# Norms of two streams staggered, and adaLN vectors moved to VectorE, in a hybrid backbone kernel

## The chip, the core and the metric

The kernel runs on one core of a Trainium2 chip. The metric is the device time of one execution, in microseconds, the median of several runs. Engine names in the profile: PE is the matrix engine (TensorE), PEld its weight load, DVE is VectorE, ACT is ScalarE, POOL is GpSimd, SP issues the DMAs.

## The reference

Two layers work on 512 tokens of width 1024: 256 latent tokens (stream 0) and 256 context tokens (stream 1). Every sub-layer modulates its input with adaLN vectors that come from a conditioning vector, one for each stream, and ends in a layer norm:

```python
def macaron_ffn(h, shift, scale, gate, w_in, w_out, g, b):
    y = swiglu(modulate(h, shift, scale), w_in, w_out)       # silu(a) * b, hidden width 2816
    return layer_norm(DN_ALPHA * h + 0.5 * gate * y, g, b)
# layer: FFN -> mixers (HGRN2 | Hyena | windowed attention, merged by gates, one output projection) -> FFN
```

All sums are in float32. The output is the latent stream after two layers, so the second layer's mixer output and second FFN have only 256 columns.

## The kernel before, in words

Activations lie transposed: eight tiles of 128 channels by 512 tokens (`ah`), the streams side by side in the columns. A float32 product is made of three matmuls of a faster format, with weights and activations split in a high and a low part: `hi` is a rounded copy by ACT (L130), `lo` the rest by DVE (L132), and `mm3` (or L530, L531, L533 in `projO`) multiplies hi by hi, hi by lo and lo by hi. Split weights lie in three buffers of 1024 columns each for `hi` and `lo`.

An FFN runs twice over half of the hidden width. In each half 11 hidden blocks are made: two projections of 24 matmuls (a `pj` bank each), silu on ACT (L476), the product with the second bank on DVE (L477), and the split of the result (`g`). Then come eight output blocks d of 33 matmuls (L141 to L143), whose residual is added by DVE (L366). In the second half the residual also collects the sums for the norm.

`norm` then takes the token means of the sum and the squares with matmuls one column wide (L389), the mean for all columns (L423), rstd on ACT, DVE and POOL (L426), and its broadcast (L461). DVE subtracts and scales (L411, L438), ACT modulates and makes the rounded `uh` (L350, L352), DVE the rest `ul` (L357), POOL the rescaled residual (L449). While this chain runs, PE works on adaLN groups, the only work that doesn't need the normalized tokens.

One adaLN group is 512 of a layer's 9216 modulation values, for both streams. It can be made in two ways. `ada_group` lets PE multiply 8 weight slabs of 128 × 512 (L293), and PE transposes the result (L321). `ada_pairs` lets DVE multiply and add slab by slab into one accumulator for each stream (L266), two groups at a time, and PE only adds up the partitions of four accumulators with a vector of ones (L273) and transposes (L279). The second form is a generator that `pull` moves on by a step or two after each hidden block and output block. Of 36 groups, 14 go this way, 18 go by PE in the norms and at fixed places of FFNs (the `fill` table), and 4 of the first layer are made at the start.

The program is written as a list of operations, and a scheduler sets the order on each engine from its own costs; HOIST gives priority to the chains of the mixers. Inside `manual_schedule` the written order holds: in the kernel before, for PE in `norm` alone. The Hyena filters of both layers (`filters`) are made during layer 0's first FFN.

Of the kernel before, what the change touches and what calls it, by code (L numbers as in the profile page):

```python
# [16 lines left out]
P = 128  # L17
# [10 lines left out]
PAIR0 = ((6, 7), (8, 9), (13, 14))  # L28
HOLES = (3, 0, 0, 2)
BG = (2, 1)  # L30
LAG = 4
SKIP = (1, 2, 3)
# [45 lines left out]
class Net:  # L78
    def __init__(self, ctx, tc, a, out):
        self.tc, self.nc, self.a, self.out = tc, tc.nc, a, out  # L80
        self.uid = 0
        self.now, self.chains = 0.0, []
        ep = lambda **k: ctx.enter_context(tc.tile_pool(**k))
# [50 lines left out]

    def split(self, src, hi, lo):
        self.nc.scalar.activation(hi, src, AF.Copy)
        self.nc.vector.tensor_tensor(lo, src, hi, ALU.subtract)
# [32 lines left out]

    def pull(self, n):
        self.slot += 1
        if self.slot not in self.bg_skip:
            for _ in range(n):
                next(self.bg, None)
# [74 lines left out]
    def ada_pairs(self, l, gs, mods):  # L250
# [3 lines left out]
        for pair in gs:  # L254
            acc = []
            for g in pair:
                acc += [self.slab("W", name="acc") for _ in range(2)]
                for k in range(KD):
                    w = self.slab("EH"[k % 2], name="adaw")
                    nc.sync.dma_start(out=w, in_=self.a["ada_w"][l, g, k])  # L260
                    for t, s in zip(acc[-2:], range(2)):
# [5 lines left out]
                    if k % 2:  # L267
# [7 lines left out]
            sb = self.slab("T", name="ada")  # L275
            nc.scalar.activation(sb, p, AF.Copy)
            tr = self.pbank("ph")
            for b in range(4):
                nc.tensor.transpose(tr[:, b * P:(b + 1) * P], sb[:, b * P:(b + 1) * P], self.ident)  # L279
            v = tr.rearrange("p (b g s x) -> p g b s x", b=4, g=2, s=2)  # L280
            for i, g in enumerate(pair):
                bias = self.par("ada_b", l * 72 + g * 4, 4)
                nc.vector.tensor_tensor(mods[:, g * 4:g * 4 + 4, :], v[:, i, :, :, 0],
                                        bias.unsqueeze(2).to_broadcast([P, 4, 2]), ALU.add)
# [106 lines left out]
    def norm(self, l, i, ah, TT, st, mods_next, ish, keep=True, out=None, fill=()):  # L391
        nc = self.nc
        nb = TT // P
        units, end = [], None
        for f in fill:
            x = self.ada_group(*f)
            units += [(x, 1), end, (x, 1), (x, 1), (x, 1)] if end else [(x, 1)] * 4
            end = (x, 0)
        units += [end] if end else []

        def more(n):
            while units and n >= units[0][1]:
                x, m = units.pop(0)
                next(x, None)
                n -= m
# [8 lines left out]
        with self.tc.manual_schedule(engines={mybir.EngineType.PE}), self.tc.issue_after(self.last_mm.ins):  # L414
            more(HOLES[0])
            for tb in range(nb):
                self.token_mean(st["stat"][:, tb:tb + 1], st["s1"], tb, False, False)
            more(HOLES[1])
            for tb in range(nb):
                self.token_mean(st["stat"][:, 4 + tb:5 + tb], st["sq"], tb, False, tb == nb - 1)  # L420
            more(HOLES[2])
# [7 lines left out]
            more(HOLES[3])  # L429
# [25 lines left out]
        return u + [self.low(x, TT) for x in pend]  # L455
# [10 lines left out]
    def ffn(self, l, i, u, ah, TT, gate, extra=None, pre=None):  # L466
# [3 lines left out]
        hg_done = False  # L470
        for half in range(2):
            g = []

            def finish(pa, pb):
                s = self.slab("T", name="silu")
                nc.scalar.activation(s[:, :TT], pa[:, :TT], AF.Silu)  # L476
                nc.vector.tensor_tensor(s[:, :TT], s[:, :TT], pb[:, :TT], ALU.mult)  # L477
# [5 lines left out]
            while j < HALF:  # L483
# [5 lines left out]
                if n == 3:  # L489
                    banks = self.projO(pre, u, [TT] * 6)  # L490
                elif n == 2:
                    banks = self.projO([w(q) for q in range(3)], u, [TT] * 3)
                    finish(*banks[:2])
                    banks = banks[2:] + self.projO([w(3)], u, [TT], "ph")
# [5 lines left out]
                self.pull(BG[0])  # L500
# [7 lines left out]
            for d in range(KD):  # L508
                if half and d == KD - 1:
                    self.squares(st, TT)  # L510
# [8 lines left out]
                self.pull(BG[1])  # L519
# [45 lines left out]
    def hgrn_proj(self, l, h, u, NQ, outer):  # L565
        nc = self.nc
        i = 4 + 4 * h
        if outer:
            ws = [self.wload(self.a["mix_w"][l, i + q], tags=(None, "QQ", "FF")[q],
                             marks=self.marks if q in PIN else None) for q in range(3)]  # L570
            pz = self.projO(ws, u, (T, T, NQ))
        else:
            pz = [self.projT(l, i + r, u, T) for r in range(2)]
        f, k = self.wide("F", name="f"), self.wide("F", name="k")
        for r in range(2):
            col = l * 8 + r * 4 + h
            c = slice(r * T, (r + 1) * T)
            nc.scalar.activation(f[:, c], pz[r], AF.Sigmoid)
            nc.scalar.activation(k[:, c], pz[r], AF.Sigmoid, scale=-1.0)
# [3 lines left out]
        pq = pz[2] if outer else self.projT(l, i + 2, u, NQ)  # L583
        q = self.slab("S", name="q")
        nc.scalar.activation(q[:, :NQ], pq[:, :NQ], AF.Copy)
        pg = self.projT(l, i + 3, u, NQ, "ph" if outer else "pj")
# [477 lines left out]
    def mixer(self, l, u, ah, TT, gate):  # L1064
# [31 lines left out]
        def proj(h):  # L1096
            hp.append(self.hgrn_proj(l, h, u, TT, h == 0))
# [34 lines left out]
        for d in range(KD):  # L1132
            if d == KD - 1:
                self.squares(st, TT)
# [4 lines left out]
    def run(self):  # L1139
# [21 lines left out]
        for d in range(KD):  # L1161
# [7 lines left out]
            if d < 2:  # L1169
# [3 lines left out]
            (0, 0): [lz(ada, 0, 4), lz(ada, 0, 5), None, self.tables_a] + [None] * F0 + [lz(self.filters, 0)] + [None] * F1 +  # L1173
                    [self.tables_b, lz(ada, 0, 15), lz(self.filters, 1)],
            (1, 0): [None] + [lz(ada, 1, 15)],
        }
        bg = {(0, 0): self.ada_pairs(0, PAIR0, mods[0]),
              (0, 1): self.ada_pairs(1, [(1, 2), (3, 7)], mods[1]),
              (1, 0): self.ada_pairs(1, [(8, 9), (13, 14)], mods[1])}
        for l in range(DEPTH):  # L1180
            TT = T if l < DEPTH - 1 else L
            self.bg, self.slot, self.bg_skip = bg.get((l, 0), iter(())), 0, SKIP
            st = self.ffn(l, 0, u, ah, T, lambda: self.mod_cols(mods[l], 2), fill.get((l, 0)), pre if l == 0 else None)
            u = self.norm(l, 0, ah, T, st, mods[l], 3, fill=[(l, g, mods[l]) for g in (10, 11, 12)])
            st = self.mixer(l, u, ah, TT, self.mod_cols(mods[l], 5))
            u = self.norm(l, 1, ah, TT, st, mods[l], 6,
                          fill=[(l, 16, mods[l]), (l, 17, mods[l])] + ([(l + 1, 0, mods[l + 1])] if l < DEPTH - 1 else []))
            self.bg, self.slot, self.bg_skip = bg.get((l, 1), iter(())), 0, SKIP
            st = self.ffn(l, 1, u, ah, TT, lambda: self.mod_cols(mods[l], 8), fill.get((l, 1)))
            if l < DEPTH - 1:  # L1190
# [130 lines left out]
```

## Time and profile before

| | |
|---|---|
| median of 3 runs | 2385.11 us (2383.44 to 2387.33) |
| profiled execution | 2383.82 us, span 2382.0 us |
| granted PE clock, mean | 0.994 of full |
| PE, DVE, ACT, POOL busy | 98%, 60%, 41%, 7% of the span |
| PE waits for ACT's copy of adaLN sums (L321) | 9.7 us in 13 waits |
| PE waits for rstd (L461) | 3.9 us in 3 waits |
| DMA | 360.41 MB, mean 151 GB/s |

Busy time of a pipelined engine counts overlapping instructions once; the busy time of one matmul row is longer than its distance to the next, and the distance is what a matmul costs. A wait is idle time ahead of an instruction, with what ended it.

### The profile page before, as it was taken

The numbers are of one execution on the slowest core, as the hardware profiler recorded it, in microseconds if no ns is written. First come the engines' busy times: TensorE is split into PE (matmuls) and PEld (weight loads), VectorE is DVE, ScalarE is ACT, GpSimd is POOL, SyncE is SP. The second block draws the span as 40 slices with busy tenths as digits, with TensorE's granted clock in tenths as the row PEclk, the third lists the DMA queues.
The fourth block names the chain that finished last, engine by engine and source line by source line (L and its number), as shares of the span: only waits on it lengthen the run. The fifth ranks groups of instructions, "written<-read, shape, count | busy, mean of one in ns | idle before, by whom it ended". The sixth has DMA issues, their size and how long they took to land.

```text
span 2382.0 us, 34116 instructions
## 1 busy us (share of the span) xinstructions
PE 2343.4 (98%) x13112; PEld 1971.4 (83%) x13112; DVE 1440.5 (60%) x2403; ACT 970.3 (41%) x1663; POOL 170.3 (7%) x158
## 2 busy tenths in 40 slices
PE   8999999999999999999999999999999999999998
PEld 4778778699888888867888877878887999998998
DVE  3647848656877665776433357363346687776555
ACT  3424324444654433343222234222225466645443
POOL 1003002210010000010000001000002111000000
PEclk9999999999999999999999999999999999999999
DMA  9435734723223445765332247243224344694564
GB/s 365 139 102 172 233 97 121 263 67 105 77 80 128 154 137 190 254 207 156 108 121 93 83 139 251 90 149 106 92 86 137 118 129 138 197 320 153 171 198 125
DMA packets 153314, 360.41 MB, mean 151 GB/s; under 512 B 16576, under 2 KB 38208, under 8 KB 153152
## 3 DMA queue, kind: packets, MB, share of 16 engines
q1 hardware_dynamic: 153152, 358.24, 46.2%
q8 instruction: 103, 1.69, 0.3%
q14 instruction: 59, 0.48, 0.1%
HBM read 331.96 MB, written 26.21 MB: 150 GB/s over the span
## 4 chain that ended last, share of the span: by engine, by line
PE 94%; DMA 2%; DVE 2%; ACT 1%; issue 1%; SPq 1%; POOL 0%; ACTq 0%; DVEq 0%
PE pj L530 18%; PE pj L531 18%; PE pj L533 18%; PE pj L141 7%; PE pj L143 7%; PE pj L142 7%; PE ph L632 2%; PE pj L551 1%; PE pj L552 1%; PE pj L553 1%; PE ph L293 1%; PE pa L1006 1%; PE pa L873 1%; PE ph L678 1%; PE pa L997 1%
## 5 line engine op out<-in xcount | busy, mean ns | idle before, releaser
L132 DVE TENSOR_TENSOR lo<-raw,hi 128x1024 fp32r<-128x1024 f32 (+1 forms) x455 | 524.6, 1154 | 451.1 <-ACT hi L130 450.2
L530 PE MATMUL pj<-uh,hi 128*128 128x512 f32 (+1 forms) x2096 | 752.5, 359 | 4.6 <-ACT uh L352 3.0
L533 PE MATMUL pj<-ul,hi 128*128 128x512 f32 (+1 forms) x2096 | 749.2, 358 | 1.1 <-DVE ul L357 1.1
L531 PE MATMUL pj<-uh,lo 128*128 128x512 f32 (+1 forms) x2096 | 749.5, 358 | 0.0
L130 ACT ACTIVATE hi<-raw 128x1024 fp32r<-128x1024 f32 (+1 forms) x455 | 446.4, 982 | 602.3 <-issue 251.2
L530 PEld LDWEIGHTS pj<-uh,hi 128*128 128x128 f32 x2096 | 396.6, 189 | 74.5 <-issue 8.6
L533 PEld LDWEIGHTS pj<-ul,hi 128*128 128x128 f32 x2096 | 396.1, 189 | 59.3 <-DVE ul L357 2.5
L531 PEld LDWEIGHTS pj<-uh,lo 128*128 128x128 f32 x2096 | 396.4, 189 | 56.8 <-issue 2.1
L142 PE MATMUL pj<-g,hi 128*128 128x512 f32 (+1 forms) x704 | 255.7, 363 | 0.0
L143 PE MATMUL pj<-g,lo 128*128 128x512 f32 (+1 forms) x704 | 255.5, 363 | 0.0
L141 PE MATMUL pj<-g,hi 128*128 128x512 f32 (+1 forms) x704 | 255.4, 364 | 0.0
L141 PEld LDWEIGHTS pj<-g,hi 128*128 128x128 f32 x704 | 132.8, 189 | 23.7 <-issue 1.7
L143 PEld LDWEIGHTS pj<-g,lo 128*128 128x128 f32 x704 | 132.9, 189 | 22.3 <-DVE ah L366 1.7
L142 PEld LDWEIGHTS pj<-g,hi 128*128 128x128 f32 x704 | 132.9, 189 | 21.3 <-issue 0.8
L476 ACT ACTIVATE silu<-pj 128x512 f32<-128x512 f32 (+1 forms) x87 | 47.3, 543 | 244.2 <-PE pj L533 244.2
L266 DVE SCALAR_TENSOR_TENSOR acc<-adaw,sc,acc 128x512 f32<-128x512 f32 x196 | 138.2, 747 | 3.9 <-DMA adaw<-ada_w 3.5
L477 DVE TENSOR_TENSOR silu<-silu,pj 128x512 f32<-128x512 f32 (+1 forms) x83 | 51.3, 619 | 147.0 <-PE pj L533 135.7
L366 DVE SCALAR_TENSOR_TENSOR ah<-pj,hg,ah 128x256 f32<-128x256 f32 x136 | 60.3, 478 | 90.0 <-PE pj L143 70.3
L426 POOL TENSOR_TENSOR rstd<-var,mhalf 128x4 f32<-128x4 f32 (+1 forms) x6 | 6.4, 1063 | 1111.9 <-DVE var L425 1111.9
L551 PE MATMUL pj<-hi,uh 128*128 128x256 f32 x288 | 82.2, 288 | 0.2
L552 PE MATMUL pj<-lo,uh 128*128 128x256 f32 x288 | 81.9, 286 | 0.0
L553 PE MATMUL pj<-hi,ul 128*128 128x256 f32 x288 | 81.6, 286 | 0.0
(293 smaller groups left out, 3110.3 us busy)
## 6 DMA issues: line engine op xcount, KB each, us to landing
raw<-ffn_in SPq DMA_DIRECT2D x176, 512.0 KB, 3.4
adaw<-ada_w SPq DMA_DIRECT2D x256, 256.0 KB, 4.8
raw<-mix_w SPq DMA_DIRECT2D x124, 512.0 KB, 3.5
raw<-ffn_out SPq DMA_DIRECT2D x64, 384.0 KB, 3.1
raw<-ffn_out SPq DMA_DIRECT2D x64, 320.0 KB, 2.9
raw<-branch_w SPq DMA_DIRECT2D x24, 512.0 KB, 5.3
adaw<-ada_f SPq DMA_DIRECT2D x32, 256.0 KB, 6.0
raw<-out_w SPq DMA_DIRECT2D x16, 512.0 KB, 4.6
```

The lines of the kernel that those rows point to most:

```text
L130: nc.scalar.activation(hi[:, :n], raw[:, :n], AF.Copy)
L132: nc.vector.tensor_tensor(lo[:, :n], raw[:, :n], hi[:, :n], ALU.subtract)
L141: nc.tensor.matmul(out, lhsT=wh, rhs=xh, start=start, stop=False)
L142: nc.tensor.matmul(out, lhsT=wh, rhs=xl, start=False, stop=False)
L143: self.last_mm = nc.tensor.matmul(out, lhsT=wl, rhs=xh, start=False, stop=stop)
L266: nc.vector.scalar_tensor_tensor(t, w, c, t, ALU.mult, ALU.add)
L530: self.nc.tensor.matmul(p, lhsT=hi, rhs=u[k][0][:, :n], start=(k == 0), stop=False)
L531: self.nc.tensor.matmul(p, lhsT=lo, rhs=u[k][0][:, :n], start=False, stop=False)
L533: self.last_mm = self.nc.tensor.matmul(p, lhsT=hi, rhs=u[k][1][:, :n], start=False, stop=(k == KD - 1))
L551: nc.tensor.matmul(o, lhsT=u[k][0][:, s], rhs=hi[:, c], start=(k == 0), stop=False)
L552: nc.tensor.matmul(o, lhsT=u[k][0][:, s], rhs=lo[:, c], start=False, stop=False)
L553: nc.tensor.matmul(o, lhsT=u[k][1][:, s], rhs=hi[:, c], start=False, stop=(k == KD - 1))
```

## The change

1. At four norms (layer 0: FFN to mixer, mixer to FFN, FFN to the next layer's FFN; layer 1: FFN to mixer) a new function `seam` takes the place of the last two output blocks (three in the mixer), of `norm`, and of the first three projections of the next stage. All of it is done for stream 0 and then for stream 1, with 256 columns instead of 512: products of stream 0; products of stream 1, with stream 0's statistics, centres and rstd among them; the three projections ("heads") of stream 0, with stream 1's statistics among them; the heads of stream 1. The order on PE, DVE and ACT is the written one there (SEAM). The fourth projection keeps 512 columns.
2. The groups by DVE rise from 14 to 26, in twelve sets of four accumulators each, alternately in the slab classes W and E; those by PE fall from 18 to 6. Accumulations (now L297) go from 196 to 336. The sums (L314, in `ada_sum`) are taken while the next set runs, at its step 6, in written order on PE.
3. The steps come at a fractional rate (PULL), none in slots 1 and 2, and none in three slots from the eighth (first FFN) or the twelfth (second FFN of layer 0); what is left is drawn at output block 3 of the second half. The filters of layer 1 move to the second FFN of layer 0, second half.
4. The last two norms (layer 1) keep their form; their adaLN groups stand at other places among the statistics.

```diff
-            for _ in range(LAG):
-                yield
-            p = self.pbank("ph")
-            for q, t in enumerate(acc):
-                nc.tensor.matmul(p[32 * q:32 * q + 32, :], lhsT=self.ones, rhs=t, start=True, stop=True,
+        for i, (l, part) in enumerate(gs):
...
+                acc += [self.slab("WE"[i % 2], name="acc") for _ in range(ns)]
...
+                    if k % (4 // ns) == 4 // ns - 1:
+                        n += 1
+                        if n == LAG and old:
+                            self.ada_sum(*old, mods)
                         yield
+            old, n = (l, part, acc), 0
+    def ada_sum(self, l, part, acc, mods):
...
+        with self.tc.manual_schedule(engines={mybir.EngineType.PE}):
+            for q in (3, 2, 1, 0):
+                nc.tensor.matmul(p[32 * q:32 * q + 32, :], lhsT=self.ones, rhs=acc[q], start=True, stop=True,
+                                 tile_position=(0, 32 * q))
+        sb = self.slab("T", name="ada")
+        nc.scalar.activation(sb, p, AF.Copy)
+        tr = self.pbank("ph")
+        for b in range(4):
+            nc.tensor.transpose(tr[:, b * P:(b + 1) * P], sb[:, b * P:(b + 1) * P], self.ident)
```

The core of `seam` (statistics, centres and operands are the norm's, for one stream):

```diff
+        with self.tc.manual_schedule(engines=SEAM), self.tc.issue_after(self.last_mm.ins):
+            for s in range(2):
+                n = 0
+                for d, ops in prods:
+                    p = self.pbank("pj")
+                    for k, (wh, wl, xh, xl) in enumerate(ops):
+                        self.mm3(p[:, :L], wh, wl, xh[:, cols(s)], xl[:, cols(s)], k == 0, k == len(ops) - 1)
+                        n += s
+                        if n == STATS:
+                            stats(0)
+                        elif STATS < n <= STATS + KD:
+                            center(n - STATS - 1, 0)
+                        elif n == STATS + KD + 1:
+                            R[0] = self.bcast(rstd[0], 2, "pa")
+                    if not s or d < KD - 1:
+                        self.residual_of(d, p, gate, ah, st, s)
+            for s in range(2):
...
+                for k in range(KD):
+                    if k < KD - 1:
+                        next(x[k + 1])
+                    next(x[k])
...
+                    for y, p in zip(w, banks):
+                        self.last_mm = nc.tensor.matmul(p[:, :L], lhsT=y[k][0], rhs=xl, start=False, stop=(k == KD - 1))
+                    if not s:
+                        if k == 0:
+                            self.residual_of(KD - 1, last, gate, ah, st, 1)
+                        elif k == 2:
+                            stats(1)
+                        elif 2 < k < KD - 1:
+                            center(2 * k - 6, 1)
+                            center(2 * k - 5, 1)
+                        if k == 5:
+                            R[1] = self.bcast(rstd[1], 2, "pa")
```

```diff
+        bg = {(0, 0): ([(0, g) for g in ((6, 7), (8, 9), (12, 13), (14, 15))], F0 + 5),
+              (0, 1): ([(0, (16, 17)), (1, (0, 1)), (1, (2, 3)), (1, (4, 5))], 12),
+              (1, 0): ([(1, g) for g in ((6, 7), (8, 9), (10, 11, 12, 13), (14, 15))], 0)}
```

In the rows of the order a number behind a name marks the tile; `pj` and `ph` are PSUM banks. PE at the third norm (layer 0's second FFN to layer 1), before, from the token means to the first projection:

```order
L389 MATMUL pa_11715<-onesD,S_11452 128x1 x4
L389 MATMUL pa_11715<-onesD,sq_11768 128x1 x4
L423 MATMUL pa_11803<-S_11452,onesD 128x512
L293 MATMUL ph_11776<-adaw_11814,sc 32x512
L293 MATMUL ph_11776<-adaw_11817,sc 32x512
L293 MATMUL ph_11820<-adaw_11821,sc 32x512
L293 MATMUL ph_11820<-adaw_11824,sc 32x512
L321 MATMUL ph_11829<-prm,ada_11827 128x128 x4
L461 MATMUL pa_11836<-prm,rstd_11773 128x128 x4
```

The same place after the change: the statistics of stream 0 (L430, L515) stand between products of stream 1, and 27 product matmuls later comes the broadcast (L618):

```order
L163 MATMUL pj_12354<-g_11450,wl_12217 128x256
L430 MATMUL pa_12370<-onesD,sq_11947 128x1 x2
L430 MATMUL pa_12370<-onesD,sq_12351 128x1 x2
L430 MATMUL pa_12370<-onesD,S_11999 128x1 x2
L515 MATMUL pa_12377<-S_11999,onesD 128x256
L161 MATMUL pj_12354<-g_11534,wh_12216 128x256
...
L163 MATMUL pj_12414<-g_11263,wl_12233 128x256
L618 MATMUL pa_12426<-prm,rstd_12381 128x128 x2
L161 MATMUL pj_12414<-g_11347,wh_12232 128x256
```

No adaLN group is left there; 24 more product matmuls follow before the first head.

PE at adaLN sums, before, in the second half of layer 0's first FFN: the scheduler set the four sums apart, between projections:

```order
L533 MATMUL pj_2278<-ul_483,hi_2274 128x512
L273 MATMUL ph_2309<-acc_1701,ones 32x512
L530 MATMUL pj_2347<-uh_201,hi_2343 128x512
L531 MATMUL pj_2347<-uh_201,lo_2344 128x512
L533 MATMUL pj_2347<-ul_202,hi_2343 128x512
L273 MATMUL ph_2309<-acc_1702,ones 32x512
```

After, near the end of layer 0's second FFN, with the transposes (L320) straight behind:

```order
L717 MATMUL pj_11836<-ul_9314,hi_11832 128x512
L314 MATMUL ph_11744<-acc_11351,ones 32x512
L314 MATMUL ph_11744<-acc_11350,ones 32x512
L314 MATMUL ph_11744<-acc_10890,ones 32x512
L314 MATMUL ph_11744<-acc_10889,ones 32x512
L320 MATMUL ph_11754<-prm,ada_11752 128x128 x4
L714 MATMUL pj_11867<-uh_9176,hi_11863 128x512
```

The four sums stand together in the middle of the last hidden block, 72 matmuls after the last of bank pj_11712.

DVE at the end of layer 0's second FFN, before, from the silu product of the second hidden block from the end to the last:

```order
L477 TENSOR_TENSOR silu_11276<-silu_11276,pj_11251 128x512
L132 TENSOR_TENSOR lo_11356<-raw_11353,hi_11355 128x768
L137 TENSOR_TENSOR g_11280<-silu_11276,g_11279 128x512
L132 TENSOR_TENSOR lo_11380<-raw_11377,hi_11379 128x640
L477 TENSOR_TENSOR silu_11345<-silu_11345,pj_11320 128x512
```

After: behind the silu product of bank pj_11712, DVE has 32 accumulations, four `lo` and a `g` up to the last accumulation of acc_11351, the one that the sum above waits for. The first and last rows:

```order
L642 TENSOR_TENSOR silu_11737<-silu_11737,pj_11712 128x512
L297 SCALAR_TENSOR_TENSOR acc_12929<-adaw_12935,sc,acc_12929 128x512
L297 SCALAR_TENSOR_TENSOR acc_12930<-adaw_12935,sc,acc_12930 128x512
L297 SCALAR_TENSOR_TENSOR acc_11350<-adaw_11364,sc,acc_11350 128x512
L135 TENSOR_TENSOR lo_11833<-raw_11830,hi_11832 128x1024
...
L297 SCALAR_TENSOR_TENSOR acc_13100<-adaw_13186,sc,acc_13100 128x512
L297 SCALAR_TENSOR_TENSOR acc_11351<-adaw_11465,sc,acc_11351 128x512
L297 SCALAR_TENSOR_TENSOR acc_12929<-adaw_13023,sc,acc_12929 128x512
```

Before, two `lo` and a `g` stood between two silu products and no accumulation; now accumulations of four sets (two of them, from acc_12929 on, of the next layer) stand there, and the next silu product, of bank pj_11798, comes 12 accumulations behind the row of acc_11351. In layer 0's first FFN the like stands behind bank pj_2163: 32 accumulations, five `lo`, two silu products and two `g`, up to the last that the sum of acc_1866 waits for, 120 matmuls later on PE.

## Rows read from the trace of the kernel before

**Rows 1.** The page's first part: busy time, share of the span, instructions.
```profile
PE 2343.4 (98%) x13112; PEld 1971.4 (83%) x13112; DVE 1440.5 (60%) x2403; ACT 970.3 (41%) x1663; POOL 170.3 (7%) x158
```

**Rows 2.** Windows, the four norms (first, last, sum): length; busy PE, PEld, DVE...; clock.
```profile
441.60:462.10 20.50, 16.50 (x92) 7.38 (x91) 13.04 (x23) 8.00 (x13) 5.09 (x5) 0.83 0.82 297
...
1803.10:1818.10 15.00, 13.58 (x92) 6.35 (x91) 11.77 (x22) 6.92 (x12) 3.34 (x5) 1.00 0.80 278
sum 67.20, PE 57.85 PEld 26.29 DVE 47.64 ACT 31.29 POOL 15.14; mean PE 14.46 PEld 6.57 DVE 11.91 ACT 7.82 POOL 3.78
```

**Rows 3.** Timeline of PE, third norm: start, busy us, engine, line, operation, count.
```profile
1423.71 1.05 PE L389 MATMUL pa<-onesD,S 128*128 128x1 f32 x8
1424.63 1.03 PE L389 MATMUL pa<-onesD,sq 128*128 128x1 f32 x8
1425.52 1.10 PE L423 MATMUL pa<-S,onesD 128*128 128x512 f32 x2
1426.56 1.07 PE L293 MATMUL ph<-adaw,sc 128*32 128x512 f32 x8
1428.33 0.66 PE L321 MATMUL ph<-prm,ada 128*128 128x128 f32 x4 [0.71 <-ACT ada L318]
1428.83 1.06 PE L461 MATMUL pa<-prm,rstd 128*128 128x128 f32 x8
1429.81 1.92 PE L293 MATMUL ph<-adaw,sc 128*32 128x512 f32 x16
```

**Rows 4.** Timeline of PE, a steady run of 512 columns, 29 matmuls apart.
```profile
1452.61 0.39 PE L530 MATMUL pj<-uh,hi 128*128 128x512 f32 x1
...
1459.18 0.39 PE L533 MATMUL ph<-ul,hi 128*128 128x512 f32 x1
```

**Rows 5.** Timeline of PE, a burst of two adaLN sums.
```profile
270.78 1.04 PE L273 MATMUL ph<-acc,ones 128*32 128x512 f32 x2
```

**Rows 6.** Timeline of PE, a steady run of 256 columns, 8 matmuls apart.
```profile
2163.67 0.28 PE L531 MATMUL pj<-m,lo 128*128 128x256 f32 x1
...
2164.63 0.28 PE L530 MATMUL pj<-m,hi 128*128 128x256 f32 x1
```

**Rows 7.** Timeline of DVE, accumulations in a row.
```profile
281.18 1.22 DVE L132 TENSOR_TENSOR lo<-raw,hi 128x1024 fp32r<-128x1024 f32 x1
282.32 4.72 DVE L266 SCALAR_TENSOR_TENSOR acc<-adaw,sc,acc 128x512 f32<-128x512 f32 x7
286.96 0.68 DVE L477 TENSOR_TENSOR silu<-silu,pj 128x512 f32<-128x512 f32 x1
```

**Rows 8.** Groups by line, the accumulations: busy us, mean ns, idle before.
```profile
L266 DVE SCALAR_TENSOR_TENSOR acc<-adaw,sc,acc 128x512 f32<-128x512 f32 x196 | 138.2, 747 | 3.9 <-DMA adaw<-ada_w 3.5 <-ACT acc L264 0.4
```

**Rows 9.** Timeline of DVE, 256 columns (last norm but one).
```profile
2180.18 0.41 DVE L438 TENSOR_TENSOR t<-t,pa 128x256 f32<-128x256 f32 x1
2180.51 0.41 DVE L411 TENSOR_TENSOR t<-ah,pa 128x256 f32<-128x256 f32 x1
```

**Rows 10.** Timeline of ACT, 256 columns, one operand to the next.
```profile
2178.02 0.59 ACT L350 ACTIVATE u<-t,B,G 128x256 f32<-128x256 f32 x1
...
2178.97 0.59 ACT L350 ACTIVATE u<-t,B,G 128x256 f32<-128x256 f32 x1
```

**Rows 11.** Timeline of DVE, the same operation twice.
```profile
465.01 0.94 DVE L357 TENSOR_TENSOR ul<-u,uh 128x512 fp32r<-128x512 f32 x1
...
469.08 0.68 DVE L357 TENSOR_TENSOR ul<-u,uh 128x512 fp32r<-128x512 f32 x1
```

**Rows 12.** Timeline of POOL beside the first of them.
```profile
464.64 0.78 POOL L449 TENSOR_SCALAR ah<-t,alg,alb 128x512 f32<-128x512 f32 x1 [1.38 <-DVE t L438]
```

**Rows 13.** Timeline of ACT, first norm's end.
```profile
471.35 1.28 ACT L578 ACT_TABLE_LOAD   x1
```

**Rows 14.** Timeline of PE, first norm.
```profile
453.27 2.08 PE L461 MATMUL pa<-prm,rstd 128*128 128x128 f32 x8 [2.58 <-POOL rstd L426]
```

**Rows 15.** Windows, the 6 us behind that wait (columns as in rows 2).
```profile
453.00:459.00 6.00, 5.65 (x24) 2.38 (x24) 3.62 (x7) 0.62 (x2) 2.54 (x4) 0.50 0.47 162
```

More of the change, by code (lines that the diff above doesn't have):

```diff
@@ L169, in drain, with begin @@
             self.step(c)
+    def begin(self, bg, units, hold=0):
+        self.held = set(range(1, SKIP + 1)) | set(range(hold, hold + HOLD) if hold else ())
+        self.bg, self.units, self.slot, self.due = bg, units * 8 + LAG + 1, 0, 0.0
     def pull(self, n):
         self.slot += 1
-        if self.slot not in self.bg_skip:
-            for _ in range(n):
-                next(self.bg, None)
+        if self.slot in self.held:
+            return
+        self.due += n
+        while self.due >= 1.0:
+            self.due -= 1.0
+            next(self.bg, None)
     def setup(self):
@@ L393, in norm @@
         nb = TT // P
[L394 to L399, printed above, removed]
-        def more(n):
[L402 to L405, printed above, removed]
+        groups = [[self.ada_group(*f), KD // 2] for f in fill]
+        def more(n):
+            for x in groups:
+                while n and x[1]:
+                    next(x[0])
+                    x[1] -= 1
+                    n -= 1
         c = []
@@ L428, in norm @@
                 center(d)
-            more(HOLES[3])
+            more(2)
             R = self.bcast(rstd, nb, "pa")
@@ L457, in bcast, with end_groups @@
+    def end_groups(self):
+        for x in self.ends:
+            next(x, None)
+        self.ends = []
     def bcast(self, cols, nb, tag):
@@ L463, in bcast, with ffn @@
         return p
-    def ffn(self, l, i, u, ah, TT, gate, extra=None, pre=None):
+    def ffn(self, l, i, u, ah, TT, gate, extra=None, pre=None, heads=None, seam=None):
         nc, a = self.nc, self.a
@@ L518, in ffn @@
                 self.residual(d, p, hg, ah, TT, st, half == 1)
-                self.pull(BG[1])
+                if d == 3 and half:
+                    for _ in self.bg:
+                        pass
+                elif d < 3 or not half:
+                    self.pull(rate * PULL[1])
         return st
@@ L1062, in merge, with mixer @@
         return res
-    def mixer(self, l, u, ah, TT, gate):
+    def mixer(self, l, u, heads, ah, TT, gate, seam):
         nc = self.nc
@@ L1180, in run @@
+        heads = None
         for l in range(DEPTH):
             TT = T if l < DEPTH - 1 else L
[L1182 to L1187, printed above, removed]
@@ new lines, in run @@
+            r = self.mixer(l, u, heads, ah, TT, self.mod_cols(mods[l], 5),
+                           None if last else dict(i=1, mods=mods[l], ish=6, **ffn_head(l, 1)))
+            u, heads = r if not last else (self.norm(l, 1, ah, TT, r, mods[l], 6, fill=[(l, g, mods[l]) for g in (16, 17)]),
+                                           None)
+            background(l, 1)
+            r = self.ffn(l, 1, u, ah, TT, lambda: self.mod_cols(mods[l], 8), fill.get((l, 1)), None, heads,
+                         None if last else dict(i=2, mods=mods[l + 1], ish=0, **ffn_head(l + 1, 0)))
@@ L1192, in run @@
+            if last:
+                self.norm(l, 2, ah, TT, r, None, 0, out=self.out)
             else:
-                self.norm(l, 2, ah, TT, st, None, 0, out=self.out)
+                u, heads = r
 def _cols(v):
```

239 lines of the change are left out of this document (180 added, 59 removed).

## The prediction

> **What bounds the kernel now.** I read the page's first lines first: PE is busy 98% of the span, VectorE (DVE) 60%, ScalarE (ACT) 41% [rows 1]. So a microsecond that leaves PE's queue is a microsecond of time, as long as no other engine takes PE's place. Then I read the windows of PE between the last product of a stage and the first `uh` matmul of the next, at the four norms that the change rewrites: 67.20 us together, the longest 20.50 and the shortest 15.00, and PE is busy in 57.85 of them [rows 2]. The third norm, row by row, shows with what: adaLN groups (L293), token means (L389), the mean (L423), the broadcast of rstd (L461) [rows 3]. Last I read the steady paces of PE, DVE and ACT, and then the order of the changed program, for what stands in PE's queue and what it needs. The profiled execution took 2383.82 us and its span 2382.0, 1.8 outside the span; it is 1.3 below the median 2385.11. The sum is made against 2383.8.
>
> **The four norms.** All four stretches leave PE's queue: −67.2. The adaLN work in them goes to DVE, and the small matmuls come back inside the products and heads: six token-mean columns, a mean and two broadcast columns for each stream, per norm as many in all as before. By the third norm: three L389 groups at 0.92, 0.89 and, taken alike, 0.9 make 2.7; the mean 1.04; the broadcast 0.98 [rows 3]. That is 4.7. Cutting them in two costs PE about four more entries into small matmuls. A burst of L273 with two matmuls is busy for 1.04, as long as eight columns are in rows 3, so it is the entry that costs, and not the count [rows 3, 5]; four entries with a part of that each I take at 1.1. 5.8 per norm, +23.2 (19 to 27).
>
> **Halved columns.** In the order 534 fp32r matmuls of 512 columns go and 1068 of 256 come. 29 matmuls of 512 from 1452.61 to 1459.18 give 0.2266 each, 8 of 256 from 2163.67 to 2164.63 give 0.120 [rows 4, 6]. 534 × (0.240 − 0.2266) = +7.2.
>
> **adaLN sums.** Before, 56 column sums stand in 15 bursts, of about 1.0 us even for two [rows 5], and with seven sets of transposes; after, 48 in 12 unbroken bursts and with twelve sets, at 0.4 each, a little under the 0.50 of L321 in rows 3. −3 × 1.0 + 5 × 0.4 = −1.0 (−2 to 0). The fill groups 4, 5, 15, 15 become 4, 5, 10, 11: 0. The last layer's two norms change only the order of the same matmuls: 0 (±1).
>
> **Inside a seam.** Stream 0's heads give PE 9 matmuls per k, 9 × 0.120 = 1.08 us. DVE has, per operand, the multiply and `ul`, and in four of the eight steps two centres as well: 4 × 0.33 = 1.32 [rows 9]. ACT makes one operand in 0.95 [rows 10]. So PE waits 4 × 0.24 = 1.0 per seam; I take 1.5 with the statistics (0 to 5): +6.0. The stages behind: entering a mixer, ACT must load a table, 1.28 [rows 13], and take eight 256-column sigmoids before it splits more weights, while all three weight buffers were held by the heads. PE has w3's 24 matmuls, 5.4 us, partly spent among the heads. I take 2.7 at the first mixer, 1.8 at the second, 0 at the FFNs: +4.5 (0 to 10).
>
> A neighbour matters here: `ul` of 512 columns took 0.94 where POOL ran its rescale beside it and 0.68 alone [rows 11, 12], so 0.13 at 256 columns; it is in the 1.5. The Trainium skill, "SBUF — State Buffer", section "Who interferes with whom", says that a DVE instruction with two SBUF inputs and a GpSimd instruction that reads SBUF lock each other out for the whole instruction. By that rule the operand would wait out POOL's half-size rescale, an estimate of 0.4 of the 0.78 in rows 12, and the seams would cost some 9 us more; the trace shows 0.26 of 0.78, so the sum goes by the row.
>
> **The sums' places.** This decides. Accumulations rise from 196 to 336. Seven of them took from 282.32 to 286.96, 0.663 each; a 1024-column `lo` 1.14; silu is busy for 0.68, and g has the same shape [rows 7]. A hidden step of an FFN is 48 matmuls, 10.9 us, and DVE has room for eight accumulations beside 2 × 1.14 + 2 × 0.68. But the Hyena filters push accumulations back, and the order shows them packed at two places, with the sum (L314) in PE's queue at a fixed place. It cannot slip behind other matmuls as L273 could.
>
> Second FFN of layer 0, last steps: from the end of bank pj_11712, PE has 72 matmuls to the sum, 16.3 us. DVE has, up to the last accumulation that it needs, 32 accumulations, two 1024-column `lo`, one of 768 and one of 640 (0.86 and 0.71 by width), one silu, one g: 21.2 + 2.3 + 1.6 + 1.4 = 26.5. PE waits 10.2. Transposes stand right behind the sum, and wait for ACT's copy: 0.7. Then DVE, still behind, needs 22 accumulations, two silu, one g, a 768-column `lo` and small ones (17.8) before `lo_11953`, due at 44.3. PE reaches it after 16.3 + 10.9, 1.4 for the sum and its transposes, and 24 and 33 matmuls (12.9), at 41.5: 2.8. Together 13.7.
>
> First FFN, half 1: from bank pj_2163, 120 matmuls, 27.2, against 32 accumulations, five `lo`, two silu and two g, 29.6: 2.4, and 0.7 for the copy. The other ten sums stand one to four steps behind their accumulations: 0. Sum +16.8; from below 0, if the accumulations come sooner; from above 24, if each takes the mean busy time of 0.747 instead of the 0.663 of a packed run (86 × 0.084 = 7) [rows 8].
>
> A PE that stood still pays again. After it waited 2.58 us for rstd [rows 14], its clock was 0.50 of full, the 1.2 GHz level, over the next 6 us [rows 15]: 3.0 lost. The wait of 10.2 us has the same: +3.0. The Trainium skill, "TensorE: Matmul & The Clock Gate", section "Part 1: The HAM clock gate", says that idling throttles the array and sustained activity releases it; rows 14 and 15 agree. By that rule the seams' short waits could each cost this too, which would make the seams the slower rival's.
>
> **Sum.** −67.2 + 23.2 + 7.2 − 1.0 + 6.0 + 4.5 + 16.8 + 3.0 = −7.5: 2376.3 against the profiled run, 2377.6 against the median; I say 2377.
>
> **Rivals.** *The sums don't wait.* Before, DVE was packed too, with seven accumulations in a row between a `lo` and a silu [rows 7], and PE's 98% leaves little that could have waited [rows 1]. If that holds, 16.8 and 3.0 go from the sum: 2357. Against it: those sums were not tied to a place, and PE's queue cannot pass a waiting instruction.
>
> *The operand chain sets the pace in the seams* (slower). DVE, ACT and the seam's PE run in written order, so a late operand stops all three. If a step of stream 0 takes 1.32 + 2 × 0.13 = 1.58 at all eight k instead of 1.08, that is 4.0 per seam for the 1.5 above, and the half clock adds 3.0: 5.5 × 4 = +22, 2398. It decides from the point where an operand takes DVE over 1.08. For it: DVE is busy for 11.77 of 15.00 in the last such stretch now [rows 2]; against it: only four of eight steps carry centres.
>
> *The accumulations come later than DVE's pace.* 32 of them need 16 slabs of 256 KB, 4.2 MB, and the hidden steps beside them 1 MB per 10.9 us: 6.6 MB in 26.5 us, 249 GB/s, where a norm stretch moves 278 to 297 [rows 2]. If a slab is late once, another 10 us: 2386, no change.
>
> *It doesn't do what it says*: the stagger leaves a stretch without PE work at each norm. The order puts twenty-odd matmuls between a stream's statistics and their use, so I leave that in the second rival.
>
> **Chances.** Forecast 0.44 (its own range 2367 to 2386), sums that don't wait 0.17, operand chain 0.22, late slabs 0.17. The measurement tells apart about 0.2%, 4.8 us: faster is below 2380.3, slower above 2389.9. Faster: 0.325 of the forecast, 0.165 of the first rival, 0.02 of the third: 0.51. Same: 0.10 + 0.02 + 0.10 = 0.22. Slower: 0.27. Range 2356 (the first rival) to 2399 (the second).
>
> **What would show it.** The norm stretches gone, and each seam with 5 to 6 us of small matmuls and under 2 of waits; L314 of the second FFN of layer 0 waiting 10 us for `acc`, with a clock of 0.5 behind it, and about 2 in the first FFN; no other sum that waits. If no L314 waits, the first rival holds; if PE waits for `uh` or `ul` at each k of a seam, the second; if an accumulation waits for `adaw` there, the third. An adaLN sum that waits at the other ten places, or a mixer entrance over 10 us, would make the forecast wrong in a way that no rival has.

## The result: 0.5% slower, and the profile after

The changed kernel takes 2396.71 us (median of 5 runs, 2394.03 to 2403.15) against 2385.11; the ratio is 1.0052, 95% interval 1.0035 to 1.0069. The forecast was 2377, 0.3% faster; the slower side had 0.27. The profiled execution took 2394.03, its span 2392.0, 10.0 longer than before.

From both traces, cut at the same pieces of work on PE (a seam here runs from the start of the last two or three output products to the end of the next stage's fourth projection):

| stretch | before | after | difference |
|---|---|---|---|
| layer 0, first FFN up to its last two blocks | 413.9 | 412.1 | −1.8 |
| seam 1 | 57.8 | 45.6 | −12.2 |
| mixer of layer 0 | 533.7 | 552.6 | **+18.9** |
| seam 2 | 56.9 | 46.7 | −10.2 |
| layer 0, second FFN | 329.9 | 359.5 | **+29.6** |
| seam 3 | 54.5 | 45.2 | −9.3 |
| layer 1, first FFN | 328.7 | 329.2 | +0.5 |
| seam 4 | 47.6 | 42.6 | −5.0 |
| rest | 546.3 | 545.8 | −0.5 |

The four stretches of [rows 2] are gone. The seams gave 36.7, and more than that was lost between them. (The filters of layer 1 left the first FFN and came into the second: between the two kernels of experiment 4, which have no accumulations, the first row of this table is 11.7 shorter, 390.7 against 402.4. So the first FFN lost some 10 beside that, and the second some 18.)

What PE waited for, after; line, releaser, us in total, times, longest:

```profile
PE ph L314 <- DVE acc L297: 20.8, 2, 12.7
PE pj L161 <- DVE gate L1246: 8.1, 6, 2.2
...
PE pa L618 <- POOL rstd L462: 3.1, 2, 2.4
...
PE pj L714 <- DVE gate L1246: 2.2, 2, 2.0
PE ph L320 <- ACT ada L317: 1.6, 2, 0.8
```

The first line is the two sums that the prediction named, the last the transposes behind them. The lines with `gate` are in the mixer of layer 0, and were not foreseen.

The second of the sums, on PE (start, busy us) and, in the fence after it, DVE's queue ahead of it:

```profile
1373.89 1.94 PE L314 MATMUL ph<-acc,ones 128*32 128x512 f32 x8 [12.66 <-DVE acc L297]
1376.63 1.11 PE L320 MATMUL ph<-prm,ada 128*128 128x128 f32 x4 [0.80 <-ACT ada L317]
1377.39 0.78 PE L714 MATMUL pj<-uh,hi 128*128 128x512 f32 x1
```

```profile
1347.47 0.68 DVE L642 TENSOR_TENSOR silu<-silu,pj 128x512 f32<-128x512 f32 x1
1348.07 2.07 DVE L297 SCALAR_TENSOR_TENSOR acc<-adaw,sc,acc 128x512 f32<-128x512 f32 x3
...
1357.57 4.07 DVE L297 SCALAR_TENSOR_TENSOR acc<-adaw,sc,acc 128x512 f32<-128x512 f32 x6
1361.54 0.96 DVE L135 TENSOR_TENSOR lo<-raw,hi 128x768 fp32r<-128x768 f32 x1
1362.41 5.39 DVE L297 SCALAR_TENSOR_TENSOR acc<-adaw,sc,acc 128x512 f32<-128x512 f32 x8
1367.71 0.83 DVE L135 TENSOR_TENSOR lo<-raw,hi 128x640 fp32r<-128x640 f32 x1
1368.45 6.05 DVE L297 SCALAR_TENSOR_TENSOR acc<-adaw,sc,acc 128x512 f32<-128x512 f32 x9
```

DVE runs without a gap from the silu product to the sum's last accumulation: 1347.47 to about 1373.8, 26.3, where the prediction had 26.5 from rows of before [rows 7]. But PE reached the sum at 1361.23 (1373.89 − 12.66), so 72 matmuls earlier is 1344.9: the silu product itself was 2.6 late behind other accumulations, and the wait was 12.7 instead of 10.2.

In the first FFN DVE stood still before the crowd (start, busy us, idle before):

```profile
246.88 2.08 DVE L297 SCALAR_TENSOR_TENSOR acc<-adaw,sc,acc 128x512 f32<-128x512 f32 x3 [7.00 <-DMA adaw<-ada_w]
...
253.33 0.68 DVE L642 TENSOR_TENSOR silu<-silu,pj 128x512 f32<-128x512 f32 x1
```

PE was at that sum at 274.6, and 120 matmuls before that is 247.4. The accumulations whose weights came late (7.00 idle) stand ahead of the silu product, which so ran 5.9 late; the wait was 8.15 and not 2.4.

Behind both waits PE ran at the lower of its two levels, as after the wait in [rows 14, 15] (windows; length, busy by engine, clock):

```profile
282.70:289.00 6.30, 5.48 (x21) 1.46 (x22) 6.30 (x9) 2.03 (x4) 0.00 (x0) 0.50 0.83 280
1373.80:1380.00 6.20, 5.31 (x19) 3.05 (x20) 6.20 (x11) 1.58 (x3) 0.00 (x0) 0.52 0.85 267
```

In the mixer the loss lies in the merge. Windows of 78 us there (columns as in [rows 2]), after and then before:

```profile
935.00:1013.00 78.00, 65.47 (x260) 49.67 (x259) 76.82 (x116) 25.78 (x36) 0.00 (x0) 0.96 0.84 288
```

```profile
925.00:1003.00 78.00, 77.03 (x348) 63.73 (x347) 52.14 (x72) 24.69 (x31) 2.20 (x1) 1.00 0.78 273
```

DVE is busy for 76.82 of the 78 us where it had 52.14, and PE for 65.47 where it had 77.03. The groups of DVE by line in the same windows (count, busy us), after and then before:

```profile
L297 DVE SCALAR_TENSOR_TENSOR acc<-adaw,sc,acc 128x512 f32<-128x512 f32 x56 | 39.8, 736 | 0.8 <-ACT acc L295 0.8
...
L1248 DVE TENSOR_TENSOR gate<-gate,gate 128x512 f32<-128x512 f32 x16 | 10.8, 674 | 0.0
L1246 DVE SCALAR_TENSOR_TENSOR gate<-gate,pj 128x512 f32<-128x512 f32 x16 | 10.7, 670 | 0.0
```

```profile
L1057 DVE TENSOR_TENSOR gate<-gate,gate 128x512 f32<-128x512 f32 x16 | 10.9, 688 | 0.3
L1055 DVE SCALAR_TENSOR_TENSOR gate<-gate,pj 128x512 f32<-128x512 f32 x16 | 10.9, 684 | 7.0 <-DMA gate<-gd 6.8 <-PE pj L143 0.2
```

56 accumulations, the first two sets of the *next* FFN, lie in the merge. Nothing in the program ties them to their own FFN, so the scheduler could put them there (experiment 1 ties them). They stand in front of gate products, which read the PSUM banks that PE wants to fill again (DVE, then PE):

```profile
965.11 2.06 DVE L297 SCALAR_TENSOR_TENSOR acc<-adaw,sc,acc 128x512 f32<-128x512 f32 x3
967.10 0.67 DVE L1246 SCALAR_TENSOR_TENSOR gate<-gate,pj 128x512 f32<-128x512 f32 x1
```

```profile
966.14 0.39 PE L163 MATMUL pj<-y,lo 128*128 128x512 f32 x1
967.91 0.47 PE L161 MATMUL pj<-y,hi 128*128 128x512 f32 x1 [1.38 <-DVE gate L1246]
```

PE's waits from the end of the mixer's entrance to its last products make 12.5 us, for gates, `hi` and `lo`; with the granted clock of 0.96 over 78 us, an estimate of 3 more, that is most of the loss.

The seams have few waits that the profile lists. Windows of the first three, after, and their sum before:

```profile
424.80:470.40 45.60, 45.01 (x337) 42.10 (x335) 27.72 (x69) 24.57 (x52) 13.53 (x21) 1.00 0.28 93
...
sum 137.50, PE 136.04 PEld 127.80 DVE 88.77 ACT 70.94 POOL 37.35; mean PE 45.35 PEld 42.60 DVE 29.59 ACT 23.65 POOL 12.45
```

```profile
sum 169.20, PE 160.18 PEld 113.06 DVE 123.70 ACT 77.80 POOL 35.36; mean PE 53.39 PEld 37.69 DVE 41.23 ACT 25.93 POOL 11.79
```

But the heads do wait for their operands, mostly in pieces too short for the table of waits (PE, first seam):

```profile
445.02 0.28 PE L581 MATMUL ph<-ul,hi 128*128 128x256 f32 x1
445.43 0.39 PE L578 MATMUL pj<-uh,hi 128*128 128x256 f32 x1
445.65 0.28 PE L579 MATMUL pj<-uh,lo 128*128 128x256 f32 x1
```

The matmuls start 0.41 and 0.22 apart there instead of 0.120, because `uh` comes late. Added up over the starts of all heads, such pieces cost 2.3, 2.2, 2.3 and 5.1 us in the four seams, 11.8 together. In the fourth one wait is long enough to be listed, and PE's granted clock behind it is 0.61 on average:

```profile
1836.37 0.39 PE L578 MATMUL pj<-uh,hi 128*128 128x256 f32 x1 [1.28 <-ACT uh L535]
```

```profile
1836.30:1840.70 4.40, 4.33 (x21) 4.12 (x22) 3.92 (x9) 4.22 (x9) 3.11 (x4) 0.61 0.38 121
```

The small matmuls are cheaper than forecast; a broadcast for one stream, in PE's row of products:

```profile
439.38 0.28 PE L163 MATMUL pj<-g,wl 128*128 128x256 f32 x1
439.50 0.60 PE L618 MATMUL pa<-prm,rstd 128*128 128x128 f32 x4
439.86 0.36 PE L161 MATMUL pj<-g,wh 128*128 128x256 f32 x1
```

0.36 for the broadcast, with its entry. All such rows of this seam (434.50 to 436.08, 446.61 to 448.19, and two broadcasts) make 3.9; the second product behind each also starts late, by 0.08 to 0.19, and with that it is 4.4 in each of the four seams, where the sum had 5.8.

### The profile page after: what moved, and what is told of

It reads as the page before. It is cut to its first block, busy times and chain, and to the rows that moved or that the text cites. A ratio compares the mean times of both kernels' runs of the same rounds, so it can differ in the third digit from the quotient of the medians.

```text
span 2392.0 us, 35248 instructions
## 1 busy us (share of the span) xinstructions
PE 2329.0 (97%) x13474; PEld 1998.9 (84%) x13474; DVE 1532.2 (64%) x2662; ACT 994.5 (42%) x1749; POOL 181.5 (8%) x194
## 5 line engine op out<-in xcount | busy, mean ns | idle before, releaser
L135 DVE TENSOR_TENSOR lo<-raw,hi 128x1024 fp32r<-128x1024 f32 (+2 forms) x444 | 512.4, 1155 | 378.8 <-ACT hi L133 378.3
L714 PE MATMUL pj<-uh,hi 128*128 128x512 f32 (+1 forms) x2064 | 740.1, 359 | 2.8 <-ACT uh L393 2.8
L717 PE MATMUL pj<-ul,hi 128*128 128x512 f32 (+1 forms) x2064 | 736.4, 358 | 0.0
L133 ACT ACTIVATE hi<-raw 128x1024 fp32r<-128x1024 f32 (+2 forms) x444 | 437.4, 988 | 541.3 <-PE pj L162 225.3
L297 DVE SCALAR_TENSOR_TENSOR acc<-adaw,sc,acc 128x512 f32<-128x512 f32 x336 | 232.4, 743 | 9.3 <-DMA adaw<-ada_w 8.4
L161 PE MATMUL pj<-g,hi 128*128 128x512 f32 (+1 forms) x638 | 229.7, 361 | 0.0
L163 PE MATMUL pj<-g,lo 128*128 128x512 f32 (+1 forms) x638 | 229.5, 360 | 0.0
L162 PE MATMUL pj<-g,hi 128*128 128x512 f32 (+1 forms) x638 | 229.3, 360 | 0.0
L161 PEld LDWEIGHTS pj<-g,hi 128*128 128x128 f32 x638 | 120.4, 189 | 20.4 <-ACT hi L133 1.7
L163 PEld LDWEIGHTS pj<-g,lo 128*128 128x128 f32 x638 | 120.5, 189 | 18.4 <-DVE lo L135 0.3
L162 PEld LDWEIGHTS pj<-g,hi 128*128 128x128 f32 x638 | 120.5, 189 | 17.9
L161 PE MATMUL pj<-y,hi 128*128 128x512 f32 (+1 forms) x192 | 66.2, 345 | 8.1 <-DVE gate L1246 8.1
```

What stands on the lines that cost most here:

```text
L133: nc.scalar.activation(hi[:, :n], raw[:, :n], AF.Copy)
L135: nc.vector.tensor_tensor(lo[:, :n], raw[:, :n], hi[:, :n], ALU.subtract)
L161: nc.tensor.matmul(out, lhsT=wh, rhs=xh, start=start, stop=False)
L162: nc.tensor.matmul(out, lhsT=wh, rhs=xl, start=False, stop=False)
L163: self.last_mm = nc.tensor.matmul(out, lhsT=wl, rhs=xh, start=False, stop=stop)
L297: nc.vector.scalar_tensor_tensor(t, w, c, t, ALU.mult, ALU.add)
```

## The experiments

The theory from here on (A): the seams gain, and what is lost comes from accumulations that stand in DVE's queue in front of work that PE needs. The rival (B) is named in each expectation.

**1. The mixer.** A set's first accumulation (a copy on ACT) is put behind the last operand of the seam ahead, for the second FFN of layer 0 alone:

```diff
-                            nc.scalar.activation(t, w, AF.Copy, scale=c)
+                            with self.tc.issue_after(self.behind.ins) if gs[0] == (0, (16, 17)) else ExitStack():
+                                nc.scalar.activation(t, w, AF.Copy, scale=c)
```

> The first accumulation of each set of layer 0's second FFN may not be issued before the last operand of the seam ahead of it; nothing else changes. Theory A (56 accumulations of that FFN, put ahead into the mixer's merge, make DVE the bound there): the mixer of layer 0 falls from 552.8 us to 534 to 536, its waits for gates from 10 us to 1, the total to about 2378; the two waits of the sums (8.2 and 12.7 us) stay within 3 us. Theory B (the merge is late because the seam's early weights are split there by DVE and ACT, and loaded beside the gates): the mixer stays above 548, the total within 5 us of the changed kernel's 2396.7.

2387.43 us (10 runs); the ratio to before is 1.0006 (95% interval 0.9996 to 1.0016, as in the other experiments). The mixer fell from 552.6 to 535.4, so 17 of the 19 us that it had lost were the accumulations (A). But half came back: the FFN that now has to make all four sets grew by 8.9, and the sums waited longer:

```profile
PE ph L315 <- DVE acc L298: 22.6, 2, 14.0
```

The total that A expected, 2378, was wrong.

**2. The second sum.** The same gate for layer 1's first FFN alone (`gs[0] == (1, (6, 7))`).

> The same for layer 1's first FFN alone: its accumulations no longer stand between those that the last sum of layer 0's second FFN needs; 18 of the 32 leave DVE's queue ahead of it. Theory A (that sum waits because DVE's queue is filled): its wait falls from 12.7 us to under 2, the half clock behind it goes too, the total to 2379 to 2384. Theory B (it waits because the filters push back the accumulations that it needs, or because their weights come late): the wait stays above 8, the total above 2391.

2386.22 us (10 runs), 1.0001 (0.9992 to 1.0010). Of the sums' two waits only the first FFN's is left; the gates of the mixer still wait:

```profile
PE pj L161 <- DVE gate L1247: 12.1, 8, 3.1
PE ph L315 <- DVE acc L298: 8.1, 1, 8.1
```

So without the 18 accumulations of the next layer in front of it that wait is gone (A). The FFN became 15.4 shorter, the next one, which now makes its own, 5.9 longer; the total is 2 above the expected range.

**3. The sums later.**

```diff
-LAG = 6
+LAG = 8
```

> Each sum is taken two steps later (8 instead of 6). Theory A (a sum that stands too early waits, and DVE catches up by itself): the two waits fall from 20.8 us to under 4, the total to 2370 to 2376. Theory B (DVE is overloaded there, and what doesn't wait at the sum waits for g or lo a little later): the waits at the sums fall, others grow by as much, the total stays within 6 us of 2396.7.

2378.70 us (10 runs), 0.9973 (0.9962 to 0.9984). No sum waits any more; waits for `lo` and for gates do:

```profile
PE pj L161 <- DVE gate L1246: 9.7, 7, 3.7
...
PE pj L163 <- DVE lo L135: 4.2, 2, 3.6
```

18 us less, where the waits and their half clock promised 21 to 27; the time lies between the two theories, 2.7 above A's range and well below B's. The part of B that came is in the second FFN: it takes 353.1 instead of 359.5, 6.4 less, where the wait alone was 12.7, and it now waits 4.2 for `lo`. The mixer, where the gates wait as in the changed kernel, took 3.1 longer.

**4. No accumulations,** in the changed kernel and in the kernel before (`bg = {}`, and the vectors of those groups set to zero, so that this part of the computation is left out).

> All 26 adaLN groups by DVE are left out (their vectors are zeros), with their weights, sums and transposes; the seams stay. Theory A (the seams themselves gain, and all that is lost comes from the accumulations): waits at the sums 0, mixer of layer 0 at 534, total 2396.7 - 19 - 21 - 6 (half clock) - 16 (12 sums and transposes) = 2335, between 2325 and 2345. Theory B (the seams or what they move lose part of it): total above 2355.

> The kernel before without its 14 adaLN groups by DVE (their vectors are zeros). Theory A: accumulations in that kernel cost only their 15 bursts of sums and 7 sets of transposes, 18 us: total 2365 to 2370; the changed kernel without its own (2327.1) is 38 to 43 below, which is what the seams give by the stages' lengths (37.5). Theory B (accumulations cost much there too): total under 2355, and the seams give less than 30.

2327.12 us (4 runs, 2325.49 to 2328.66) and 2356.39 (4 runs, 2352.03 to 2359.49). The changed kernel is in A's range. The kernel before is in neither: its total is above B's limit of 2355, but the difference of 29.3 is what B said of the seams (less than 30), and A is wrong there. Without accumulations the changed kernel is 29.3 faster: that is what the change gives without its DVE groups, less than the 36.7 of the stretches above. Part of the difference is that the kernel before gets shorter norms too: its seam 1 takes 53.2, from 415.15 to 468.35, instead of 57.8, without the wait of 2.58 for rstd [rows 14], and at a clock of 1.00 instead of 0.94. Why that wait is gone was not tested, nor was the rest taken apart. And 14 groups cost the kernel before 28.7 us, not the 18 that A had given them; 26 cost the changed one 69.6.

**5. Both gates.** `if self.behind` in place of the condition in 1.

> Both gates at once: the first accumulations of the second FFN of layer 0 and of the first FFN of layer 1 stand behind the last operand of the seam ahead. Theory A (the accumulations cost time only where they stand in front of work that PE needs): the gains of the two single gates add, the mixer of layer 0 at 536 to 540 us, the second FFN of layer 0 at 346 to 352, the sum's wait there under 2; total 2366 to 2374. Theory B (DVE's work is only pushed on, as the first gate alone gave back half of its gain in the FFN): total above 2380.

2374.25 us (10 runs), 0.9963 (0.9951 to 0.9974), 0.25 above A's range and far from B's. The two gates alone had gained 9.3 and 10.5; together they gain 22.5, so the gains add. Mixer 534.1; second FFN 352.3, 16.1 shorter than with the first gate alone (354.6 from the last head, as the expectation counts, 2.6 above its range). The first FFN's sum still waits 7.7, and the starts of both gated FFNs wait for `lo`, 2.0 and 1.5, likely since all accumulations that the gate held are ready at once; that was not tested.

**6. The layer-1 filters and the pause.** The pause at slots 12 to 14 of layer 0's second FFN lies among output blocks of its first half; the filters come at slot 20.

```diff
-              (0, 1): ([(0, (16, 17)), (1, (0, 1)), (1, (2, 3)), (1, (4, 5))], 12),
+              (0, 1): ([(0, (16, 17)), (1, (0, 1)), (1, (2, 3)), (1, (4, 5))], 20),
```

> The changed kernel with the pause of layer 0's second FFN at slot 20, where the filters of layer 1 stand, instead of slot 12. Theory A (the pause missed the filters, and the sum that waited 12.7 us waited for accumulations that the filters held up): that wait falls under 3 us, the total to 2378 to 2386; the mixer's 19 us and the first FFN's wait stay. Theory B (the crowding there comes from the next FFN's accumulations, which no slot holds): the wait or others in its place stay above 8 us, the total above 2390.

2383.38 us (10 runs), 0.9993 (0.9984 to 1.0003). The wait of 12.7 is gone, 8.6 in the first FFN is all:

```profile
PE ph L314 <- DVE acc L297: 8.6, 1, 8.6
```

As A expected. The sum also stands 18 product matmuls (4 us) later in PE's order, too little by itself to hide 12.7. Experiment 2 ended the same wait without touching the pause. So the wait seems to have needed both, accumulations that run into the filters and those of the next FFN in front of them: taking away either is enough.

**7. Every group in its slot.** Each group's first accumulation behind the silu of the hidden step at which the program draws it, in all three FFNs; sums at step 8 and, in a second kernel, at step 6.

```diff
-                            nc.scalar.activation(t, w, AF.Copy, scale=c)
+                            with self.tc.issue_after(self.silu.ins) if self.silu else ExitStack():
+                                nc.scalar.activation(t, w, AF.Copy, scale=c)
...
-                            nc.scalar.activation(s[:, c], y[:, :n], AF.Silu)
+                            self.silu = nc.scalar.activation(s[:, c], y[:, :n], AF.Silu)
```

> Each group of accumulations may not begin before the silu of the hidden step at which the program draws it, in all three FFNs, and each sum is taken at step 8: no accumulation runs ahead of its slot. Theory A: no wait for acc, none above 1 us for gates, the mixer of layer 0 near 536, the FFNs near those without accumulations plus 1.4 us per sum (409 + 345 + 331 against 404 + 339 + 325 when they are left out): total 2345 to 2355. Theory B (26 groups are too much for DVE wherever they stand): waits for g, lo or gates take their place, total above 2365.

> As the kernel with every group held to its slot, but with each sum at step 6, as in the changed kernel. Theory A (the slots alone end the crowding; what is left at step 6 is the wait behind the filters): two waits for acc, about 8 us in the first FFN and 3 in the second, with some half clock: total 2368 to 2376. Theory B (with the slots kept, step 6 is late enough): no wait over 1 us, total within 4 us of 2358.3.

Step 8: 2358.29 us (4 runs), 0.9893 (0.9866 to 0.9920). Step 6: 2370.83 (4 runs), 0.9939 (0.9922 to 0.9955). At step 8 no accumulation is waited for; at step 6 two waits remain, 7.6 and 4.3. Step 6 is as A said. Step 8 is 3 above A's range, a gate of the mixer waits 2.5 where A had none above 1, and the first FFN stands out: 407.0 against 390.7 without accumulations (419.7 as the expectation counts, from the start of the span, where it had 409). The profiled execution is the slowest of the four, 2364.39, so its lengths may be some microseconds too long. The trace shows part of the reason. PE's own adaLN groups 10 and 11, two bursts of 16 matmuls without accumulations, are torn into eleven (the first four of them):

```profile
293.00 1.06 PE L335 MATMUL ph<-adaw,sc 128*32 128x512 f32 x6
294.65 1.05 PE L335 MATMUL ph<-adaw,sc 128*32 128x512 f32 x2
296.52 1.04 PE L335 MATMUL ph<-adaw,sc 128*32 128x512 f32 x2
297.92 1.04 PE L335 MATMUL ph<-adaw,sc 128*32 128x512 f32 x2
```

A burst of 2 is busy for as long as one of 6. All groups by PE in that stretch take 16.4, from the first matmul of each burst to the next product, in 15 bursts; without accumulations they take 8.4 in 5, with the same 64 matmuls.

**8. PE's groups ahead of the filters.**

```diff
-            (0, 0): [lz(ada, 0, 4), lz(ada, 0, 5), None, self.tables_a] + [None] * F0 + [lz(self.filters, 0)] + [None] * 5 +
-                    [lz(ada, 0, 10), lz(ada, 0, 11), self.tables_b],
+            (0, 0): [lz(ada, 0, 4), lz(ada, 0, 5), lz(ada, 0, 10), self.tables_a, lz(ada, 0, 11)] + [None] * (F0 - 1) + [lz(self.filters, 0)] +
+                    [None] * 7 + [self.tables_b],
```

> As the kernel with every group held to its slot, and the two groups that PE makes in layer 0's first FFN (10 and 11) moved from steps 14 and 15 to steps 3 and 5, ahead of the filters. Theory A (in the kernel with the slots these groups stood in 15 bursts instead of the 5 that they have without accumulations, because both draw on the same weight slabs; a burst costs about 0.7 to 1 us whatever its size): 6 or 7 bursts, 7 us less, total 2349 to 2353, below both kernels. Theory B (the bursts cost only what their matmuls cost): total within 3 us of 2358.3.

2351.24 us (4 runs, 2350.51 to 2353.46): 0.9860 of before (0.9846 to 0.9875), faster than both kernels. The groups are whole again:

```profile
82.65 1.92 PE L335 MATMUL ph<-adaw,sc 128*32 128x512 f32 x16
96.14 1.92 PE L335 MATMUL ph<-adaw,sc 128*32 128x512 f32 x16
120.52 1.92 PE L335 MATMUL ph<-adaw,sc 128*32 128x512 f32 x16
```

That is in A's range, 7 us below the kernel of experiment 7, with six bursts. It is 24 us above the kernel without accumulations. The twelve sums stand in 15 bursts there, with twelve sets of transposes; at 0.98 to 1.00 and 0.35 to 0.39 they make 19 of that, and 23 with the late start of the second product behind each.

## Why the prediction was wrong

**The step that failed** is "The sums' places. This decides": it priced the added accumulations only where a sum waits for them. Those that stand in front of DVE's other work were put at nothing, and the mixer of layer 0 had no term but its entrance (2.7). 56 accumulations ran ahead into its merge, where no sum is near. DVE was busy for 76.82 of 78 us there, PE waited for gates, and the mixer took 18.9 longer, 17.2 of it by the accumulations (experiment 1). They were not looked for outside the FFNs. The sentence "The other ten sums stand one to four steps behind their accumulations: 0" came true, since no other sum waited, and none of the signs under "What would show it" points at the merge.

**The two waits** were rightly placed and sized too small: 8.15 and 12.66 instead of 2.4 and 10.2. DVE's own time was right (26.3 against 26.5); the count began with an idle DVE at the silu product, and DVE was 5.9 and 2.6 late there. So the first rival (the sums don't wait) did not happen. The seven idle microseconds for `adaw` in the first FFN are a small piece of the third rival (late slabs). The wait of 2.8 for `lo` behind the second sum did not come: from 1376 to the end of that FFN only the transposes wait, 0.8.

**The half clock** was 3.0 for one wait; there were two, each with a stretch at 0.50 to 0.52 of full, and the mixer's short waits had a mean of 0.95 from 943 to 1013. Of the seams only the fourth, with the wait of 1.28, has a lower clock; the first three have 1.00.

**The seams** gave 36.7, where the sum had 67.2 − 23.2 − 7.2 − 6.0 − 4.5 = 26.3. The kind was right and the sizes were not. The small matmuls cost 4.4 per seam, 17.7 in all, not 23.2. Late operands cost 11.8 in all, not 6.0. And the four stretches of the table had 73.7 us beyond the steady pace of their products and projections before, not only the 67.2 of [rows 2]; after, 30.0 are left. The entrance of the first mixer took 0.9, in two waits, not 2.7. The second rival, on whose side the result lies, came in small: it added 5.5 per seam to the sum's 1.5, and about 1.5 was added.

POOL's neighbourhood cost little: `ul` took 0.42 to 0.48 in the seams, but for one of 0.67. The prediction read its row of 0.68 as `ul` alone [rows 11], but POOL's rescale began while that one ran, and took 1.60 instead of 0.78 [rows 12]:

```profile
469.33 1.60 POOL L449 TENSOR_SCALAR ah<-t,alg,alb 128x512 f32<-128x512 f32 x1 [1.38 <-ACT u L350]
```

So in these two pairs the instruction that began second took longer. In the seams the two overlap by 0.2 us or less in most steps; where it is more, POOL's rescale took up to 1.35 instead of 0.55, and PE never waits for it.

Two small readings were off without a part in the sum: a hidden step leaves room for some eleven accumulations by the prediction's own numbers (10.9 − 2 × 1.14 − 2 × 0.68, at 0.663), not eight, and its 56 column sums of before are records, two for each of 28 matmuls.

**In the sum:** −7.5 was forecast, +10.0 came in the profiled runs: +18.9 for the mixer, which had no term; +9.5 in the FFNs, for larger waits and the second half clock; −10.4 from the seams; −0.5 in the rest. The range held the time by luck: it reached to 2399 for the second rival's sake, and the mixer filled it. The sign was wrong.

**What it would have taken.** By the kernels without accumulations the change alone gives −29.3, near the seam terms of the sum (−26.3), and DVE's groups went from 28.7 to 69.6, +41, of which +18.8 (16.8 + 3.0 − 1.0) had been forecast.

## What to carry to other kernels

Work that a scheduler may move ahead has no place of its own: look for it in the whole order of an engine, above all in stages that seem not to be touched, and price it where it stands in front of something that the bound engine waits for. An engine that is busy for 64% of the span was the bound for 78 us here. Holding filler work to its slots was worth 26 us, and 38 with the sums two steps later, three times what the change had lost.

## What the runs showed that was not expected

What a group of column matmuls costs PE depends on its bursts more than on its matmuls. In experiment 7 a burst of 2, 4 or 6 took 0.98 to 0.99 us from its first matmul to the next product, and one of 10 or 16 took 1.84 to 1.85; so 64 of them took 8.4 us in 5 bursts and 16.4 in 15. Spreading filler thinly over PE's queue is not free. That the accumulations tore the bursts apart is shown, since the same two groups at the same place are whole without them; that they did so through the slabs that both draw on is argued only. In a PE row of 256-column products, on the other hand, a burst of four small matmuls, like the broadcast above, takes 0.36.
